# Feed-forward weight tiles placed by when the mixer's bytes come free, in a two-layer decoder trunk

## The chip, the cores and the metric
The kernel runs on one core of a Trainium2 chip. A core has a matrix engine (TensorE, PE in the profile; its weight loads are PEld), three engines for elementwise work (VectorE or DVE, ScalarE or ACT, GpSimd or POOL), and a queue engine that issues the transfers here (SyncE, SP). Each engine works through its own list of instructions in order and waits on semaphores for the others. The metric is the device time of one launch in microseconds (us).

## The reference
256 tokens of width 2048 pass through two layers. Each layer is a token mixer and a feed-forward network, both added to the residual stream after an RMS norm of their input; a last norm ends it. All is float32.

```python
def swiglu(x, w_in, w_out):
    g, u = jnp.split(x @ w_in, 2, axis=-1)
    return (jax.nn.silu(g) * u) @ w_out
# layer 0: h = h + mlstm_mixer(norm(h));  h = h + swiglu(norm(h), ...)
# layer 1: h = h + rglru_mixer(norm(h));  h = h + swiglu(norm(h), ...)
# w_in: 2048 x (2 x 5632), w_out: 5632 x 2048
```

Both mixers begin with projections of the normed input and end with a projection of 2048 to 2048 (`m_w_out`, `r_w_out`), whose result is added to the residual `h`.

## The kernel before, in words
TensorE multiplies float32 numbers in a rounded format, so each factor is split in a rounded part (hi, a cast on ScalarE) and the rest (lo, a subtraction on VectorE), and a product is three matmuls: hi x hi, hi x lo, lo x hi. Every weight comes from memory once, as a raw tile; ScalarE writes its `whi`, VectorE its `wlo`. All weight loads stand on SP, in the order of their use.

A mixer streams its weights in groups of 128 x 2 x 512 (lines 180 to 200), four buffers each for raw, hi and lo in a pool "w". Its last step is `project_out` (line 422): four quarters of 512 output columns, each a `linear_tok` (line 250) of 96 matmuls into two banks `po` (lines 258 to 260), then two adds to `h` (line 429). After each quarter the norm's work for the next part is put in a list: transposes of `h`, here `tr_f` (line 381), all through one bank, a copy with the norm's gain `c_f` (line 384), some differences (line 386) and the split of the result `p_f` (lines 206 and 207), and squares for the norm (`junk`, line 309). That of the fourth quarter (pairs 6 and 7 of the input) falls behind the projection. The transposes of the second mixer are `tr_m`, its scaled inputs `x_m`, its first projection `rec`.

A feed-forward network (`ffn`, line 671) works on 11 feature blocks j. Block j takes eight pairs of 128 input rows; for each a raw tile 128 x 4 x 512 (two loads: gate and value columns; line 233). Five pairs are plain: one cast `whi` of 128 x 2048, one subtraction `wlo`, 24 matmuls. Pairs 1, 3 and 5 use seven products instead of eight: VectorE makes sums of the raw tile (`sum`, lines 242 to 246), raw and sums are split (`whix`, `wlox`, `whit`, `wlot`), 21 matmuls. The matmuls are lines 687 to 689, into seven banks P1 to Q6, which the profile shows as `P` and `Q`. Two or three blocks of inner features (tiles `hh`, `hl`) are then projected back by `w_out`.

The tiles of a network's weights all come from one pool:

```python
def four(what, name, dtype, bufs):                        # line 202
    return pool_of("w").tile([P, 4, NB], dtype, tag=what, name=..., bufs=bufs)
```

four raw, one sum, three hi, three lo, of 8 KB a partition each. This pool is opened at the network's start (line 676), where the mixer's pools have been closed, and lies over their bytes; each tile waits for what last used those bytes (`reuse_waits="tile"`). The first raw tiles lie over the mixer's raw and hi buffers, the first `whi` over its lo buffers, the first `wlo` over the pool y. The bytes of the mixer's inner part lie above and are given back after the first quarter of its projection (`nxt.open()`, line 433); over them lies the pool "f" with the inner features.

The order of each engine's list is set by a scheduler, by priority and by when it expects tiles to be ready; splits run under `tc.high_priority(offset=AHEAD)` (lines 192, 222, 235, 240), so they are put as early as their tiles allow.

Of the kernel before, what the change touches and what calls it, by code (L numbers as in the profile page):

```python
# [9 lines left out]
F32R = mybir.dt.float32r  # L10
# [4 lines left out]
P = 128  # L15
T = 256
# [8 lines left out]
NB = 512  # L25
# [13 lines left out]
def kernel(  # L39
# [28 lines left out]
    def open_pool(key, name, bufs=1, side="left", space=None):  # L68
        kw = dict(space=space) if space is not None else dict(side=side)
        pool = tc.tile_pool(name=name, bufs=bufs, reuse_waits="tile", **kw)  # L70
        pools[key] = (pool.__enter__(), pool)
        return pools[key][0]

    def close_pools(*keys):
        for key in keys:
            pools.pop(key)[1].__exit__(None, None, None)

    def pool_of(key):
        return pools[key][0]

    def acc(name):
        return pool_of("acc").tile([P, NB], F32, tag="bank", name=name)

    def misc(name):
        return pool_of("misc" if "misc" in pools else "acc").tile([P, NB], F32, tag="bank", name=name)

    def open_mixer(n):
        open_pool("acc", f"acc_{n}", 8, space=PSUM)
        open_pool("w", f"w_{n}", 4)
        open_pool("y", f"y_{n}")  # L90
# [8 lines left out]
    h = const.tile([P, NT, D], F32, name="h")  # L99
    xv = x[0].rearrange("(b p) d -> p b d", p=P)  # L100
    raw0 = {}
# [48 lines left out]
    part, at, used = 0, 0, [0, 0, 0]  # L150
    for name, src, n in par_src:
        if part == 0 and at or at + n > P:
            part, at = part + 1, 0
# [21 lines left out]
    def run_pending():  # L175
        if pending:
            pending.pop(0)()


    def stream(w, c0, nk, ncols=NB):  # L180
# [5 lines left out]
        for kg in range(0, nk, 2):  # L186
# [12 lines left out]
            for i in range(2):  # L199
                yield kg + i, hi[:, i, 0:ncols], lo[:, i, 0:ncols]  # L200

    def four(what, name, dtype, bufs):
        return pool_of("w").tile([P, 4, NB], dtype, tag=what, name=f"{what}{name}", bufs=bufs)

    def split(hi, lo, src):
        nc.scalar.copy(hi, src)  # L206
# [20 lines left out]
    def pairs(w, j):  # L227

        wv = w.rearrange("(k p) n -> p k n", p=P)
        for p in range(NK // 2):  # L230
            raw = four("raw", f"{j}_{p}", F32, 4)
            for i, c0 in enumerate((j * NB, FF + j * NB)):
                nc.sync.dma_start(raw[:, 2 * i:2 * i + 2, :], wv[:, 2 * p:2 * p + 2, c0:c0 + NB])
            if p not in SEVENS:
                with tc.high_priority(offset=AHEAD):
                    both = halves(f"{j}_{p}", raw)
                yield p, both
                continue

            with tc.high_priority(offset=AHEAD):  # L240
                t = four("sum", f"{j}_{p}", F32, 1)
                nc.vector.tensor_tensor(
                    t[:, 0:2, :], raw[:, 1:3, :], raw[:, 3:4, :].broadcast_to([P, 2, NB]), op=ALU.add
                )
                nc.vector.tensor_tensor(t[:, 2, :], t[:, 0, :], raw[:, 2, :], op=ALU.add)
                nc.vector.tensor_tensor(t[:, 3, :], t[:, 2, :], raw[:, 0, :], op=ALU.add)
                both = halves(f"x{j}_{p}", raw, 3) + halves(f"t{j}_{p}", t)
            yield p, dict(zip(("B21", "B11", "B22", "T1", "T3", "T2", "T4"), both))
# [188 lines left out]
    def split_store(dst_hi, dst_lo, src):  # L437

        nc.scalar.copy(dst_hi, src)  # L439
        nc.vector.tensor_tensor(dst_lo, src, dst_hi.bitcast(F32), op=ALU.subtract)  # L440
# [230 lines left out]
    def ffn(layer, n, nxt):  # L671

        w = ffn_w_in[layer]
        open_pool("acc", f"acc_f{layer}", 7, space=PSUM)
        open_pool("misc", f"misc_f{layer}", 1, space=PSUM)
        open_pool("w", f"w_f{layer}")
        fp = open_pool("f", f"f{layer}")

        def opening():
            close_pools("x")  # L680
            open_pool("x", f"x_after{layer}", side="right")

        nxt.opening = opening
        if True:

            def product(o, a, b, start, stop):
                nc.tensor.matmul(o, lhsT=a[0], rhs=b[0], start=start, stop=False)  # L687
                nc.tensor.matmul(o, lhsT=a[0], rhs=b[1], start=False, stop=False)  # L688
                nc.tensor.matmul(o, lhsT=a[1], rhs=b[0], start=False, stop=stop)  # L689

            def hidden(j):

                ps = {c: acc(f"{c}_{j}") for c, _, _ in PRODUCTS}
                started = set()
                dif = fp.tile([P, 2, NB], F32, tag="dif", name=f"dif{j}")
                sg = fp.tile([P, NT, NB], F32, tag="sg", name=f"sg{j}")
                for p, ops in pairs(w, j):
                    if p not in SEVENS:

                        for c, side, a in (("Q5", 1, 1), ("P2", 0, 0), ("Q3", 1, 2), ("P4", 0, 1)):  # L700
                            for f in range(2):
                                product(ps[c], n.plain(p, f)[a], ops[2 * side + f], c not in started,
                                        p == NK // 2 - 1 and f == 1)
                                started.add(c)
                    else:
                        seven = n.seven(p)
                        for c, a, b in PRODUCTS:
                            product(ps[c], seven[a], ops[b], c not in started,
                                    p == SEVENS[-1] and c in ("P7", "P1", "Q6"))
                            started.add(c)  # L710
                    if p == SEVENS[-1]:
                        nc.scalar.copy(sg[:, 0, :], ps["P1"])
                        nc.vector.tensor_tensor(dif[:, 0, :], ps["Q6"], sg[:, 0, :], op=ALU.subtract)
                        nc.vector.tensor_tensor(dif[:, 1, :], ps["P7"], dif[:, 0, :], op=ALU.add)
                    if p > 0:
                        run_pending()
                v = fp.tile([P, NT, NB], F32, tag="v", name=f"v{j}")
                for b in range(NT):
                    nc.vector.tensor_tensor(v[:, b, :], ps["Q5"], dif[:, b, :], op=ALU.add)
                nc.vector.tensor_tensor(sg[:, 0, :], ps["P2"], sg[:, 0, :], op=ALU.add)  # L720
                nc.scalar.activation(sg[:, 0, :], sg[:, 0, :], AF.Silu, scale=n.rstd[:, 0:1])
                nc.vector.tensor_tensor(v[:, 0, :], ps["Q3"], v[:, 0, :], op=ALU.add)
                nc.vector.tensor_tensor(sg[:, 1, :], ps["P4"], dif[:, 1, :], op=ALU.subtract)
                nc.scalar.activation(sg[:, 1, :], sg[:, 1, :], AF.Silu, scale=n.rstd[:, 1:2])
                for b in range(NT):
                    nc.vector.scalar_tensor_tensor(
                        out=v[:, b, :], in0=v[:, b, :], scalar=n.rstd[:, b:b + 1], in1=sg[:, b, :],
                        op0=ALU.mult, op1=ALU.mult,
                    )
                return v  # L730

            def turn_v(v, i, hi, lo):
                pt = misc("tv").rearrange("p (f t) -> p f t", f=2)
                for f in range(2):
                    for b in range(NT):
                        nc.tensor.transpose(
                            pt[:, f, b * P:(b + 1) * P], v[:, b, (2 * i + f) * P:(2 * i + f + 1) * P], ident
                        )
                split_store(hi[:, 2 * i:2 * i + 2, :], lo[:, 2 * i:2 * i + 2, :], pt)

            for js in CHUNKS:
                hh, hl = [], []
                for i, j in enumerate(js):
                    v = hidden(j)
                    hi = fp.tile([P, 4, T], F32R, tag=f"hh{i}", name=f"hh{j}")
                    lo = fp.tile([P, 4, T], F32R, tag=f"hl{i}", name=f"hl{j}")
                    hh.append(hi)
                    hl.append(lo)
                    for a in range(2):
                        pending.append(lambda v=v, a=a, hi=hi, lo=lo: turn_v(v, a, hi, lo))  # L750
                project_out(
                    ffn_w_out[layer][js[0] * NB:(js[-1] + 1) * NB, :], 4 * len(js),
                    lambda k: (hh[k // 4][:, k % 4, :], hl[k // 4][:, k % 4, :]), nxt, js[-1] == FF // NB - 1,
                )

    n2 = Norm("m1", par["g_mix"][:, 16:32], bcast=True)
    ffn(0, n1, n2)
    close_pools("f", "w", "misc", "acc")
    open_mixer("m1")


# [165 lines left out]
            nc.sync.dma_start(ov[:, 2 * NB:4 * NB], y[:, 2 * NB:4 * NB])  # L927

    ffn(1, n3, Final("fin", None))
    close_pools("f", "w", "misc", "acc", "x")  # L930


# [29 lines left out]
```

## Time and profile before

| | us |
|---|---|
| runs | 2165.64, 2165.96, 2167.81; median 2165.96 |
| the profiled execution | 2165.18 |
| its span | 2163.4 |
| TensorE busy | 2126.7 |
| VectorE busy | 1524.6 |
| ScalarE busy | 1071.0 |
| mean granted clock of TensorE | 0.991 |

The span runs from the first to the last instruction of the profiled execution; 1.8 us of its time lie around it. Times in rows count from the span's start. A row of the timeline gives start, length, engine, line, operation, what is written and read, and how many alike were merged; in brackets the idle time of the engine before it and what ended it. The first network's products begin at 411.41, the second mixer's at 1134.72, the second network's at 1436.55.

### The profile page before, as it was taken

What the parts mean: (1) busy time and instruction counts of PE and PEld (TensorE: products, weight loads), DVE (VectorE), ACT (ScalarE), POOL (GpSimd) and SP (SyncE); (2) the same over time, 40 slices, a digit from 0 to 9 for tenths busy, and PEclk for the clock granted to TensorE, in tenths of its full rate; (3) what the DMA queues carried; (4) which work ended last, traced back from release to release, by engine and by line L of the source; (5) the groups of instructions that cost most, each with busy time, mean ns of one, the idle gap of its engine ahead of it and who ended that gap; (6) DMA issues with size and microseconds to landing.
All of it is one profiled execution on the core that took longest, in us unless ns stands there. A gap on an engine that the chain in (4) does not pass through costs nothing.

```text
span 2163.4 us, 26826 instructions
## 1 busy us (share of the span) xinstructions
PE 2126.7 (98%) x10658; PEld 1788.9 (83%) x10658; DVE 1524.6 (70%) x1486; ACT 1071.0 (50%) x1040; POOL 43.4 (2%) x62
## 2 busy tenths in 40 slices
PE   8999999899999999999999999989999999999998
PEld 7988888788888888888879999778888888888886
DVE  5655555688578758866856786768857875886685
ACT  5444445555345435544544758555434543553444
POOL 0011110000000000000000000000000000000002
PEclk9999999999999999999999999999999999999999
DMA  6556655556555655565636665555665565556563
GB/s 209 166 163 178 180 180 185 178 202 209 189 193 188 203 186 195 195 201 188 206 106 195 194 188 188 190 176 195 214 195 194 175 214 175 194 195 213 176 214 117
DMA packets 211078, 405.70 MB, mean 188 GB/s; under 512 B 14520, under 2 KB 14728, under 8 KB 210824
## 3 DMA queue, kind: packets, MB, share of 16 engines
q1 hardware_dynamic: 210808, 402.94, 57.2%
q8 instruction: 83, 1.36, 0.3%
q10 hardware_dynamic: 144, 1.05, 0.1%
q14 instruction: 43, 0.35, 0.0%
HBM read 401.84 MB, written 2.10 MB: 187 GB/s over the span
## 4 chain that ended last, share of the span: by engine, by line
PE 91%; DVE 3%; ACT 2%; DMA 2%; issue 1%; SPq 0%; POOL 0%; ACTq 0%; DVEq 0%; POOLq 0%
PE po L259 10%; PE po L258 10%; PE po L260 10%; PE P L688 7%; PE P L689 7%; PE P L687 7%; PE Q L688 6%; PE Q L689 6%; PE Q L687 6%; DMA raw<-in_ffn_w_in_dram 2%; PE rec L277 1%; PE qk L275 1%; DVE wlo L207 1%; PE qk L276 1%; PE rec L276 1%; PE o L260 1%
## 5 line engine op out<-in xcount | busy, mean ns | idle before, releaser
L206 ACT CAST whi<-raw 128x2048 fp32r<-128x2048 f32 x198 | 378.3, 1912 | 465.8 <-PE P L689 204.4
L207 DVE TENSOR_TENSOR wlo<-raw,whi 128x2048 fp32r<-128x2048 f32 x198 | 451.8, 2295 | 204.8 <-ACT whi L206 204.6
L196 DVE TENSOR_TENSOR wlo<-raw,whi 128x1024 fp32r<-128x1024 f32 (+1 forms) x225 | 273.3, 1219 | 194.0 <-ACT whi L195 193.7
L195 ACT CAST whi<-raw 128x1024 fp32r<-128x1024 f32 (+1 forms) x225 | 234.3, 1047 | 215.8 <-PE po L260 53.2
L259 PE MATMUL po<-wlo,hh 128*128 128x512 f32 x704 | 275.2, 391 | 0.0
L258 PE MATMUL po<-whi,hh 128*128 128x512 f32 x704 | 275.0, 391 | 0.0
L260 PE MATMUL po<-whi,hl 128*128 128x512 f32 x704 | 273.6, 390 | 0.0
L206 ACT CAST whit<-sum 128x2048 fp32r<-128x2048 f32 x66 | 126.2, 1913 | 161.5 <-PE P L689 94.5
L207 DVE TENSOR_TENSOR wlot<-sum,whit 128x2048 fp32r<-128x2048 f32 x66 | 151.3, 2292 | 58.9 <-ACT whit L206 58.7
L687 PE MATMUL Q<-whi,p_f 128*128 128x512 f32 x440 | 175.7, 399 | 8.5 <-ACT whi L206 8.5
L688 PE MATMUL Q<-wlo,p_f 128*128 128x512 f32 x440 | 174.1, 396 | 3.6 <-DVE wlo L207 3.6
L687 PE MATMUL P<-whi,p_f 128*128 128x512 f32 x440 | 174.0, 395 | 0.0
L689 PE MATMUL Q<-whi,p_f 128*128 128x512 f32 x440 | 172.8, 393 | 0.0
L688 PE MATMUL P<-wlo,p_f 128*128 128x512 f32 x440 | 172.7, 393 | 0.0
L689 PE MATMUL P<-whi,p_f 128*128 128x512 f32 x440 | 172.5, 392 | 0.0
L258 PEld LDWEIGHTS po<-whi,hh 128*128 128x128 f32 x704 | 132.2, 188 | 27.5 <-ACT hh L439 0.3
L259 PEld LDWEIGHTS po<-wlo,hh 128*128 128x128 f32 x704 | 132.5, 188 | 26.5
L260 PEld LDWEIGHTS po<-whi,hl 128*128 128x128 f32 x704 | 132.1, 188 | 26.9
L206 ACT CAST whix<-raw 128x1536 fp32r<-128x1536 f32 x66 | 98.0, 1485 | 80.6 <-PE P L689 53.9
L207 DVE TENSOR_TENSOR wlox<-raw,whix 128x1536 fp32r<-128x1536 f32 x66 | 115.7, 1753 | 16.8 <-ACT whix L206 16.3
L687 PEld LDWEIGHTS Q<-whi,p_f 128*128 128x128 f32 x440 | 83.4, 190 | 26.6 <-ACT whi L206 9.1
L688 PEld LDWEIGHTS Q<-wlo,p_f 128*128 128x128 f32 x440 | 83.3, 189 | 24.4 <-DVE wlo L207 7.4
(261 smaller groups left out, 4258.5 us busy)
## 6 DMA issues: line engine op xcount, KB each, us to landing
raw<-in_ffn_w_in_dram SPq DMA_DIRECT2D x352, 512.0 KB, 4.8
raw<-in_ffn_w_out_dram SPq DMA_DIRECT2D x176, 512.0 KB, 4.9
raw<-in_m_w_in_dram SPq DMA_DIRECT2D x95, 512.0 KB, 3.8
raw<-in_r_w_in_dram SPq DMA_DIRECT2D x64, 512.0 KB, 4.2
raw<-in_m_w_out_dram SPq DMA_DIRECT2D x32, 512.0 KB, 3.7
raw<-in_r_w_out_dram SPq DMA_DIRECT2D x32, 512.0 KB, 3.7
gr<-in_r_gate_w_dram SPq DMA_DIRECT2D x8, 512.0 KB, 3.8
h<-in_x_dram SPq DMA_DIRECT2D x4, 512.0 KB, 7.9
```

Source lines behind the costliest of these rows:

```text
L195: nc.scalar.copy(hi[:, i:i + step, 0:ncols], r)
L196: nc.vector.tensor_tensor(lo[:, i:i + step, 0:ncols], r, hi[:, i:i + step, 0:ncols].bitcast(F32), op=ALU.subtract)
L206: nc.scalar.copy(hi, src)
L207: nc.vector.tensor_tensor(lo, src, hi.bitcast(F32), op=ALU.subtract)
L258: nc.tensor.matmul(o, lhsT=ah[:, bs], rhs=hi, start=(k == 0), stop=False)
L259: nc.tensor.matmul(o, lhsT=ah[:, bs], rhs=lo, start=False, stop=False)
L260: nc.tensor.matmul(o, lhsT=al[:, bs], rhs=hi, start=False, stop=(k == nk - 1))
L275: nc.tensor.matmul(o, lhsT=hi, rhs=ah, start=first_in_bank, stop=False, skip_group_check=True)
L276: nc.tensor.matmul(o, lhsT=hi, rhs=al, start=False, stop=False, skip_group_check=True)
L687: nc.tensor.matmul(o, lhsT=a[0], rhs=b[0], start=start, stop=False)
L688: nc.tensor.matmul(o, lhsT=a[0], rhs=b[1], start=False, stop=False)
L689: nc.tensor.matmul(o, lhsT=a[1], rhs=b[0], start=False, stop=stop)
```

## The change
Every tile of the one pool "w" of a network gets a pool of its own, and these are opened in the order of a list. Since pools are laid out in the order of opening, the list sets which of the mixer's bytes each tile lies over. A counter for each kind takes the tiles in turn. The first raw, `whi` and `wlo` of a network are not taken from these but from the pool "f", from the tiles `h0`, `h1`, `h2`, which hold the inner features later. For that the hi and lo of a feature block, two tiles of 4 KB, become one of 8 KB. Lines below 205 move by 8 and lines behind 686 by 12: 206 and 207 are 214 and 215 in the changed kernel, 233 is 241, 687 to 689 are 699 to 701.

```diff
+    PLACES = ("raw0", "raw1", "raw2", "raw3", "sum0", "whi2", "whi0", "wlo0", "whi1", "wlo2", "wlo1")
+    turn, early = {}, {}
+
     def four(what, name, dtype, bufs):
-        return pool_of("w").tile([P, 4, NB], dtype, tag=what, name=f"{what}{name}", bufs=bufs)
+        if what in early:
+            return pool_of("f").tile([P, 4, NB], dtype, tag=early.pop(what), name=f"{what}{name}")
+        at = turn.get(what, 0)
+        turn[what] = (at + 1) % bufs
+        return pool_of(f"{what}{at}").tile([P, 4, NB], dtype, tag=what, name=f"{what}{name}")
...
-        open_pool("w", f"w_f{layer}")
+        turn.clear()
+
+        early.update(raw="h0", whi="h1", wlo="h2")
+        for place in PLACES:
+            open_pool(place, f"{place}_f{layer}")
         fp = open_pool("f", f"f{layer}")
...
-                    hi = fp.tile([P, 4, T], F32R, tag=f"hh{i}", name=f"hh{j}")
-                    lo = fp.tile([P, 4, T], F32R, tag=f"hl{i}", name=f"hl{j}")
+                    both = fp.tile([P, 2, 4, T], F32R, tag=f"h{i}", name=f"hh{j}")
+                    hi, lo = both[:, 0], both[:, 1]
...
-    close_pools("f", "w", "misc", "acc")
+    close_pools("f", *reversed(PLACES), "misc", "acc")
```

SP, in the first mixer's output projection; `raw_0` is the first pair of the first network, the other rows are the mixer's weights:

```order
 L107 DMA raw_3031<-in_m_w_out_dram 128x2x512
 L107 DMA raw_3058<-in_m_w_out_dram 128x2x512
+L241 DMA raw_0_3645<-in_ffn_w_in_dram 128x2x512 x2
 L107 DMA raw_3076<-in_m_w_out_dram 128x2x512
 L107 DMA raw_3124<-in_m_w_out_dram 128x2x512
...
 L107 DMA raw_3552<-in_m_w_out_dram 128x2x512
 L107 DMA raw_3570<-in_m_w_out_dram 128x2x512
-L233 DMA raw_0_3615<-in_ffn_w_in_dram 128x2x512 x2
```

The two loads move ahead of 23 of the mixer's 32 (in the second network ahead of 16). The cast `whi_0` of that tile moves likewise, into the projection's first quarter.

ScalarE behind the first mixer's end, before (in `whi_0`, `whix_1` and so on the number is that of the pair; `c_f_3687` and `p_f_3691` are those of pair 6, `c_f_3730` and `p_f_3734` of pair 7):

```order
L309 ACTIVATE junk,ss_f_211<-h 128x512 x2
L384 ACTIVATE c_f_3687<-tr_f_3682,cols_107 128x256 x2
L206 CAST p_f_3691<-c_f_3687 128x768
L384 ACTIVATE c_f_3730<-tr_f_3725,cols_107 128x256 x2
L206 CAST whi_0_3618<-raw_0_3615 128x2048
L206 CAST p_f_3734<-c_f_3730 128x768
L206 CAST whix_1_3653<-raw_1_3646 128x1536
L206 CAST whit_1_3657<-sum_1_3649 128x2048
L206 CAST whi_2_3697<-raw_2_3694 128x2048
```

And now (pair 6 is `c_f_3717` and `p_f_3721`, pair 7 `c_f_3760`):

```order
L317 ACTIVATE junk,ss_f_211<-h 128x512 x2
L214 CAST whix_1_3683<-raw_1_3676 128x1536
L392 ACTIVATE c_f_3717<-tr_f_3712,cols_107 128x256 x2
L214 CAST whi_2_3727<-raw_2_3724 128x2048
L214 CAST whit_1_3687<-sum_1_3679 128x2048
L214 CAST whix_3_3783<-raw_3_3776 128x1536
L214 CAST p_f_3721<-c_f_3717 128x768
L392 ACTIVATE c_f_3760<-tr_f_3755,cols_107 128x256 x2
L214 CAST whit_3_3787<-sum_3_3779 128x2048
L214 CAST whi_4_3815<-raw_4_3812 128x2048
```

The cast of pair 0 is gone from here, four casts of the weights of pairs 1 to 3 stand ahead of the split `p_f` of pair 6, and `whi_2` ahead of `whit_1`. On TensorE the 24 matmuls of pair 0 follow the last `po` matmul, where eight transposes stood; the transposes now stand, two or four at a time, between pair 1's matmuls. The start of the second network is alike.

TensorE at the end of the last quarter before the second mixer, now (`tr_m_8418` are the transposes of the third quarter's last part, `rec_0` is the second mixer's first projection):

```order
L266 MATMUL po_1_8382<-whi_8440,hh_8118 128x512
L331 MATMUL tr_m_8418<-ident,h 128x128 x4
L267 MATMUL po_1_8382<-wlo_8441,hh_8118 128x512
...
L268 MATMUL po_1_8382<-whi_8440,hh_8118 128x512
L283 MATMUL rec_0_8523<-x_m_8230,whi_8527 128x256
L284 MATMUL rec_0_8523<-x_m_8230,whi_8527 128x256
L285 MATMUL rec_0_8523<-x_m_8230,wlo_8528 128x256
L283 MATMUL rec_0_8523<-x_m_8230,whi_8527 128x256
```

These transposes stood at the third of the last 24 `po` matmuls and are now at the sixteenth, and 36 `rec` matmuls follow each other without transposes between. Ahead of it VectorE and ScalarE have the first four splits of the second mixer's weights (lines 195 and 196) before the last quarter's adds and squares, where they stood behind them.

## Rows read from the trace of the kernel before

**Rows 1.** The page, first part: busy time, share of the span, instructions.
```profile
PE 2126.7 (98%) x10658; PEld 1788.9 (83%) x10658; DVE 1524.6 (70%) x1486; ACT 1071.0 (50%) x1040; POOL 43.4 (2%) x62
```

**Rows 2.** Waits of TensorE: us in total, times, longest.
```profile
PE Q L687 <- ACT whi L206: 8.5, 2, 4.4
...
PE rec L275 <- ACT whi L195: 2.6, 1, 2.6
PE tr_f L381 <- ACT c_f L384: 2.0, 2, 1.0
```

**Rows 3.** Stretches: busy PE, PEld, DVE, ACT, POOL, then PEclk, DMA, GB/s.
```profile
408.00:412.00 4.00, 0.59 (x1) 0.50 (x2) 1.67 (x3) 3.26 (x5) 0.00 (x0) 0.50 0.84 318
...
418.00:420.00 2.00, 2.00 (x10) 1.62 (x10) 0.56 (x1) 1.40 (x1) 0.00 (x0) 1.00 0.29 35
...
1433.00:1437.00 4.00, 0.45 (x1) 0.45 (x2) 1.67 (x3) 3.13 (x4) 0.00 (x0) 0.50 1.05 395
...
1135.00:1138.00 3.00, 2.51 (x11) 2.13 (x11) 3.00 (x5) 2.51 (x3) 0.00 (x0) 0.50 0.14 10
...
1513.00:1516.40 3.40, 2.58 (x11) 1.80 (x10) 3.40 (x3) 2.20 (x2) 0.00 (x0) 1.00 0.05 6
```

**Rows 4.** Timeline of TensorE, the first network's start.
```profile
403.65 0.39 PE L260 MATMUL po<-whi,yl 128*128 128x512 f32 x1
...
406.38 0.66 PE L381 MATMUL tr_f<-ident,h 128*128 128x128 f32 x4 [1.01 <-ACT c_f L384]
411.41 0.80 PE L687 MATMUL Q<-whi,p_f 128*128 128x512 f32 x1 [4.38 <-ACT whi L206]
...
416.47 0.63 PE L689 MATMUL P<-whi,p_f 128*128 128x512 f32 x1
416.89 0.63 PE L687 MATMUL P<-whi,p_f 128*128 128x512 f32 x1
...
441.00 0.39 PE L687 MATMUL P<-whix,p_f 128*128 128x512 f32 x1
...
456.80 0.39 PE L687 MATMUL Q<-whi,p_f 128*128 128x512 f32 x1
```

**Rows 5.** Timeline of ScalarE, the first network's start.
```profile
404.88 0.63 ACT L309 ACTIVATE junk<-h 128x512 f32<-128x512 f32 x1
405.41 0.19 ACT L309 ACTIVATION_READ_ACCUMULATOR junk<-h 128x1 f32 x1
...
409.47 1.90 ACT L206 CAST whi<-raw 128x2048 fp32r<-128x2048 f32 x1
```

**Rows 6.** Timeline of VectorE, the first network's start.
```profile
411.39 2.29 DVE L207 TENSOR_TENSOR wlo<-raw,whi 128x2048 fp32r<-128x2048 f32 x1 [1.36 <-ACT whi L206]
413.60 1.22 DVE L242 TENSOR_TENSOR sum<-raw 128x1024 f32<-128x1024 f32 x1
```

**Rows 7.** Timeline of TensorE, the second network's start.
```profile
1428.79 0.39 PE L260 MATMUL po<-whi,zl 128*128 128x512 f32 x1
...
1481.88 0.39 PE L687 MATMUL Q<-whi,p_f 128*128 128x512 f32 x1
```

**Rows 8.** Timeline of TensorE, the second mixer's start.
```profile
1131.73 0.39 PE L260 MATMUL po<-whi,hl 128*128 128x512 f32 x1
1134.72 0.55 PE L275 MATMUL rec<-x_m,whi 128*128 128x256 f32 x1 [2.61 <-ACT whi L195]
...
1142.25 0.28 PE L277 MATMUL rec<-x_m,wlo 128*128 128x256 f32 x1
...
1142.59 0.28 PE L277 MATMUL rec<-x_m,wlo 128*128 128x256 f32 x1
```

**Rows 9.** Timeline of VectorE and ScalarE, the second mixer's start.
```profile
1131.47 1.37 DVE L429 TENSOR_TENSOR h<-po,h 128x512 f32<-128x512 f32 x2 [2.35 <-PE po L260]
...
1133.64 3.87 ACT L195 CAST whi<-raw 128x1024 fp32r<-128x1024 f32 x4
```

**Rows 10.** Timeline of ScalarE, inside the first mixer's output projection.
```profile
325.04 1.05 ACT L195 CAST whi<-raw 128x1024 fp32r<-128x1024 f32 x1 [1.67 <-PE po L260]
```

**Rows 11.** Timeline of VectorE, the same place.
```profile
326.12 1.22 DVE L196 TENSOR_TENSOR wlo<-raw,whi 128x1024 fp32r<-128x1024 f32 x1 [1.49 <-ACT whi L195]
```

**Rows 12.** The page, DMA issues: line, engine, count, KB each, us to landing.
```profile
raw<-in_m_w_out_dram SPq DMA_DIRECT2D x32, 512.0 KB, 3.7
```

More of the change, by code (lines that the diff above doesn't have):

```diff
@@ L929 @@
     ffn(1, n3, Final("fin", None))
-    close_pools("f", "w", "misc", "acc", "x")
+    close_pools("f", *reversed(PLACES), "misc", "acc", "x")
 _INS = [
```

## The prediction
> **What bounds the kernel now.** I read the page first. TensorE is busy for 98% of the span [rows 1], so only time in which TensorE stands still or runs slowly can be won. The list of what TensorE waits for is short [rows 2]. The longest entry is the first product of a feed-forward network that waits for its hi weights (8.5 us in two waits, one for each network); the first product of the second mixer waits 2.6 us for the same kind of cast, and transposes wait 2.0 us until their one bank has been read. The table of stretches shows the rest of the price [rows 3]: behind each of those three waits the granted clock reads 0.50, the lower of the two levels (1.2 GHz against 2.4 GHz), and comes back some microseconds after the matmuls resume. Such a stop is thus paid twice.
>
> The timelines give the size of each place. In the first network [rows 4] the last `po` matmul of the mixer starts at 403.65, eight transposes follow, the first product starts at 411.41 after a wait of 4.38 us, and its matmuls stand 0.42 us apart (416.47, 416.89) until the clock returns; afterwards they stand closer: from the start of pair 5 at 441.00 to that of the second feature block at 456.80 are 21 + 24 + 24 matmuls, 0.229 us each. Between lie 5 plain pairs of 24 matmuls and 3 pairs of 21, so 183 matmuls; at 0.229 us they need 41.9 us, and the eight transposes some 1.1 us more (four take 0.66 with their tail). From 403.88, where the next matmul could start, to 456.80 are 52.9 us. So 9.9 us are lost: 5.4 in the two waits that the rows show, 2.7 in 14 matmuls at the low clock, the rest in smaller waits and the restart. The second network is alike [rows 7]: 1429.02 to 1481.88 are 52.9 us, 9.9 lost. At the second mixer [rows 8] the last matmul starts at 1131.73 and the first 36 of the projection are done with by 1142.70, one pitch behind the row at 1142.59; 36 at 0.114 us (three from 1142.25 to 1142.59) need 4.1 us, so 6.6 are lost. All three together are 26.4 us, and that is the most that can be had here.
>
> Why the products are late is on ScalarE [rows 5]: the squares of the norm end at 405.60, then come the casts of the last two pairs of inputs, and only at 409.47 the cast of the first weight tile. It stands there because the tile it writes lies over the mixer's buffers.
>
> **The change part by part.** Nothing is added to the number of matmuls, splits or bytes; instructions move.
>
> (1) The first pair of a network now lies where the inner features will lie, over bytes of the mixer that are free after the first quarter of its output projection. Its two loads, its cast (1.90 us, [rows 5]) and its subtraction (2.29 us, [rows 6]) go into that projection. There ScalarE has an idle 1.67 us ahead of each cast of 1.05 us [rows 10], so a 1.90 us cast makes one cast late by about 0.3 us and the next ones on time again; if the weights land later than the cast's turn, up to some 3 us, which the four buffers of each kind (each group is 2.7 us of matmuls) cover. VectorE has 1.49 us ahead of each of its subtractions [rows 11]. Cost taken: 0; from both sides 0 and, without any cover, 1.9 + 2.3 us in each of two mixers, 8.4 us.
>
> (2) Then the 24 matmuls of pair 0 follow the last `po` matmul without a wait: 403.88 to 409.38. During them ScalarE does the squares and pair 1's cast and VectorE the sums of pair 1, which before began at 413.60 [rows 6] and now can at about 406.0. The wait of 4.38 us and the low clock behind it go.
>
> (3) What is late next. The transposes of pairs 6 and 7 now stand between the products of pair 1. The second four wait for the one bank as they do now, 1.01 us [rows 4]: pair 1's first three matmuls and four transposes end at 410.5, the wait at 411.5. Six more matmuls lead to 413.1. On ScalarE the cast of pair 2 (1.90) starts at 411.5 and ends at 413.4, a wait of 0.2; behind it the cast of pair 1's sums, of the same size, ends at 415.2, while TensorE has only two matmuls to do in between: a wait of 1.4. From there on 4 + 8 + 8 + 14 matmuls run to 423.0, where pair 3 starts; before, it started 114 matmuls of 0.229 us ahead of 456.80, at 430.7. Gain so far 7.7 us. In pairs 3 and 4 the sums, the cast of the sums and the next cast stand closer than now; by the same addition they make TensorE wait 0.2 + 0.95 + 0.15 us. So the second block starts at about 450.4 and 6.4 us are won in each network. As a check from VectorE: its series of sums starts 7.6 us earlier, so the gain in a network cannot be much over that unless VectorE has slack.
>
> (4) At the second mixer the first four splits of weights move ahead of the last quarter's squares and residual adds, because their buffers now lie over tiles that are let go earlier. Casts that stood at 1133.64 [rows 9] are then done before 1131.73, and rec can start as soon as its bank is free. That bank is one the last `po` tile's add reads; two adds take 1.37 us [rows 9], and the splits and the norm's last inputs are ahead of them now, so I put the first add's end at 1132.7 and TensorE's wait at 0.7 us, too short beside a long run of matmuls to expect the clock to fall. 1132.7 + 4.1 = 1136.8 against 1142.70: 5.9 us won.
>
> Sum: 6.4 + 6.4 + 5.9 = 18.7 us. The profiled execution took 2165.18 us (span 2163.4 and 1.8 around it), close to the median of 2165.96. 2165.2 - 18.7 = 2146.5.
>
> **The clock.** The assumption that carries 9 of the 18.7 us is that the new waits leave the clock up. In the rows it fell at three places, each time after TensorE had done nothing, or nothing but transposes, from the last matmul of a projection on; the shortest stop among them is the 2.61 us ahead of rec [rows 8]. The new waits are 1.0, 0.2 and 1.4 us with two to six matmuls between them, and in a stretch of the second network in which TensorE also had pauses (2.58 us busy of 3.40) the clock read 1.00 (the last of [rows 3]). So I take it to stay up, without a row that has just this pattern.
> The Trainium skill, page "TensorE: Matmul & The Clock Gate", section "A second HAM failure mode: psum-queue depth-cycling", tells of a kernel in which short pauses between groups of matmuls came often enough for the clock to go up and down, at the cost of throughput. By that rule the new start of a network would fall into the low clock again, which is rival (b); no row of before shows a fall after pauses as short as these.
>
> **The rivals.**
> (a) The waits vanish more fully than I add up: ScalarE takes the casts in time and the clock stays. Then each network wins 8 to 9 us and the mixer 6.5: 24 us, 2141 us. For it speaks that releases are not all at their latest; against it the order on ScalarE, in which three long casts follow the transposes.
> (b) The clock falls at the new pauses. 14 matmuls at 0.42 instead of 0.23 are 2.7 us [rows 4], with the restart about 3.5 for each network: 18.7 - 7 = 11.7 us, 2153.5. If the mixer's place falls too (36 matmuls of which some 24 at 0.21 instead of 0.11: 2.5 us), 2156.
> (c) The wait only moves: the splits of pairs 1 to 4 are the true limit, and TensorE waits for VectorE's series wherever pair 0 stands. Then only the low clock or little of it is won, under 4 us: 2162 to 2166. Against it: VectorE waits for ScalarE ahead of its first long subtraction [rows 6], so it isn't at its limit there.
> (d) Slower: the early cast holds ScalarE inside the mixer. ScalarE and VectorE take their work in order; if the cast of pair 0 waits for a load that is not there, every cast of the projection queues behind it, and TensorE runs dry about 3 us later. One quarter of the projection is eight such steps of 1.67 + 1.05 us, 21.8 us, so weights that come a whole quarter late would cost up to 18.8 us in each mixer. It decides the sign from 18.7 / 2 + 3, some 12.4 us of lateness in each. The loads stand among the mixer's own, which land in 3.7 us [rows 12], and what they wait for on TensorE ended with the mixer's inner part, so I give it little. At 15 us of lateness in each: 2165.2 - 18.7 + 2 x 12 = 2170.5.
>
> **How the numbers follow.** Forecast (2143 to 2150): 0.58. (a): 0.12. (b): 0.17. (c): 0.07. (d): 0.04; 0.02 is left for what I don't see, on either side. What a measurement can tell from no change is about 0.2%, 4.3 us; faster by more are the forecast, (a), (b) and a small part of (c): 0.89; the same, most of (c): 0.06; slower 0.05. The range for 8 times in 10 leaves out the far end of (a), part of (b), (c) and (d): 2139.5 to 2156.
>
> **What would show it.** In the profile after: the cast of a network's first weights some 80 us earlier than its first product, inside the projection, with no new wait of `po` behind it; the first product straight behind the last `po`; clock 1.00 through 404 to 424 of the first network; waits for c_f, whi and whit of about 1.0, 0.2 and 1.4 us in place of 4.4; the second block 6 us closer to the mixer's end; rec no more than 1 us behind the last `po`. A reading of 0.5 in these stretches would make (b) right, waits of `po` for ScalarE (d), and an unchanged distance from the mixer's end to the second block (c).

## The result, and the profile after
The changed kernel takes 2152.61 us (median of 4 runs, 2151.89 to 2154.57) against 2166.36 (4 runs, 2165.64 to 2167.81): a ratio of 0.9937, 95% interval 0.9920 to 0.9954. The forecast was 2146.5, so the sign and the range held, and 5 us of the forecast gain are missing. The profiled executions, 2165.18 and 2152.51 us, differ by 12.7 us. Cut at the same instructions (last `po` matmul, first matmul of the second feature block, last of the first 36 `rec`), in us:

| stretch | before | after | difference | forecast |
|---|---|---|---|---|
| start to the first mixer's end | 403.65 | 403.90 | +0.25 | 0 |
| first network, start to second block | 53.15 | 47.96 | -5.2 | -6.4 |
| rest of it | 674.93 | 675.79 | +0.9 | 0 |
| second mixer, first 36 `rec` | 10.86 | 5.13 | -5.7 | -5.9 |
| rest of it | 286.20 | 287.90 | +1.7 | 0 |
| second network, start to second block | 53.09 | 48.07 | -5.0 | -6.4 |
| rest and end | 681.5 | 682.0 | +0.4 | 0 |

The three places won 15.9 of the 18.7 us that were forecast for them, and 3.2 us went elsewhere. Of these 3.2, the +0.25 and the +0.9 do not come back when both kernels are profiled again (last experiment); the +1.7 does, and the +0.4 about does. What TensorE waits for now (us in total, times, longest):

```profile
PE Q L700 <- DVE wlo L215: 4.4, 6, 1.0
PE P L699 <- ACT whit L214: 4.3, 4, 1.1
PE tr_f L389 <- ACT c_f L392: 1.9, 2, 0.9
...
PE P L699 <- ACT whi L214: 1.0, 2, 0.5
...
PE rec L283 <- DVE h L437: 0.7, 1, 0.7
```

The two waits that led [rows 2], 8.5 us for whi and 2.6 for rec, are gone; new ones of at most 1.1 us stand in their place. The stretches at the three places (columns as in [rows 3]: the granted clock is the number before the DMA share):

```profile
408.00:412.00 4.00, 3.07 (x16) 2.29 (x15) 2.55 (x4) 1.04 (x3) 0.00 (x0) 1.00 1.02 346
414.00:416.00 2.00, 0.94 (x4) 0.48 (x3) 2.00 (x2) 2.00 (x2) 0.00 (x0) 1.00 0.45 172
...
1429.00:1433.00 4.00, 2.93 (x14) 2.09 (x13) 2.63 (x3) 4.00 (x3) 0.00 (x0) 1.00 0.65 248
1128.00:1132.00 4.00, 3.33 (x30) 3.31 (x30) 1.98 (x6) 1.84 (x5) 0.73 (x2) 1.00 0.52 186
```

All are at 1.00 where [rows 3] had 0.50. TensorE at the first network's start, after:

```profile
403.90 0.39 PE L268 MATMUL po<-whi,yl 128*128 128x512 f32 x1
404.13 0.39 PE L699 MATMUL Q<-whi,p_f 128*128 128x512 f32 x1
...
411.86 0.44 PE L389 MATMUL tr_f<-ident,h 128*128 128x128 f32 x2 [0.93 <-ACT c_f L392]
...
415.44 0.50 PE L699 MATMUL P<-whit,p_f 128*128 128x512 f32 x1 [1.06 <-ACT whit L214]
...
426.98 0.50 PE L699 MATMUL P<-whi,p_f 128*128 128x512 f32 x1 [0.48 <-ACT whi L214]
...
438.45 0.50 PE L699 MATMUL P<-whit,p_f 128*128 128x512 f32 x1 [1.06 <-ACT whit L214]
...
451.86 0.39 PE L699 MATMUL Q<-whi,p_f 128*128 128x512 f32 x1
```

The first product follows the last `po` without a gap; before, 7.8 us lay between [rows 4]. Four small waits remain. Behind each, the next matmuls stand 0.34 us apart once or twice instead of 0.23. ScalarE shows where the waits for `whit` come from:

```profile
410.96 0.84 ACT L392 ACTIVATE c_f<-tr_f,cols 128x256 f32<-128x256 f32 x2 [3.73 <-PE tr_f L389]
411.69 1.90 ACT L214 CAST whi<-raw 128x2048 fp32r<-128x2048 f32 x1
413.49 1.90 ACT L214 CAST whit<-sum 128x2048 fp32r<-128x2048 f32 x1
...
434.69 1.91 ACT L214 CAST whi<-raw 128x2048 fp32r<-128x2048 f32 x1 [5.64 <-PE P L701]
436.51 1.89 ACT L214 CAST whit<-sum 128x2048 fp32r<-128x2048 f32 x1
```

Ahead of both stands the cast of the next pair. The sums that the first `whit` casts were ready at 410.4, where VectorE's last addition for them ended; their cast started 3.1 us later, behind `c_f` and `whi`.

The early cast inside the mixer's projection, ScalarE and then VectorE:

```profile
325.83 1.91 ACT L214 CAST whi<-raw 128x2048 fp32r<-128x2048 f32 x1 [2.21 <-DMA raw<-in_ffn_w_in_dram]
327.65 1.99 ACT L195 CAST whi<-raw 128x1024 fp32r<-128x1024 f32 x2
```
```profile
327.78 2.29 DVE L215 TENSOR_TENSOR wlo<-raw,whi 128x2048 fp32r<-128x2048 f32 x1 [2.89 <-ACT whi L214]
329.99 3.49 DVE L196 TENSOR_TENSOR wlo<-raw,whi 128x1024 fp32r<-128x1024 f32 x3
```

The cast waits for its load, and two of the mixer's casts and three of its subtractions then follow back to back; before, each had idle time ahead of it [rows 10, 11]. TensorE has no wait in this projection; in that of the second mixer it has 1.3 us in three short ones, as before (1.2). The second mixer's start, against [rows 8]:

```profile
1127.65 0.39 PE L268 MATMUL po<-whi,hh 128*128 128x512 f32 x1
1128.72 0.36 PE L283 MATMUL rec<-x_m,whi 128*128 128x256 f32 x1 [0.68 <-DVE h L437]
...
1132.78 0.28 PE L285 MATMUL rec<-x_m,wlo 128*128 128x256 f32 x1
```

### The profile page after: what moved, and what is told of

It reads as the page before. It is cut to its first block, busy times and chain, and to the rows that moved or that the text cites. A ratio compares the mean times of both kernels' runs of the same rounds, so it can differ in the third digit from the quotient of the medians.

```text
span 2150.7 us, 26823 instructions
## 1 busy us (share of the span) xinstructions
PE 2120.3 (99%) x10658; PEld 1784.2 (83%) x10658; DVE 1523.7 (71%) x1486; ACT 1070.3 (50%) x1040; POOL 45.1 (2%) x62
## 5 line engine op out<-in xcount | busy, mean ns | idle before, releaser
L266 PE MATMUL po<-whi,hh 128*128 128x512 f32 x704 | 275.0, 391 | 0.0
L268 PE MATMUL po<-whi,hh 128*128 128x512 f32 x704 | 273.6, 390 | 0.0
L266 PEld LDWEIGHTS po<-whi,hh 128*128 128x128 f32 x704 | 132.2, 188 | 27.6 <-ACT hh L447 0.3
L268 PEld LDWEIGHTS po<-whi,hh 128*128 128x128 f32 x704 | 132.1, 188 | 26.8
L699 PEld LDWEIGHTS P<-whi,p_f 128*128 128x128 f32 x440 | 82.6, 188 | 20.3 <-ACT whi L214 2.5
```

The lines of the kernel that those rows point to most:

```text
L266: nc.tensor.matmul(o, lhsT=ah[:, bs], rhs=hi, start=(k == 0), stop=False)
L268: nc.tensor.matmul(o, lhsT=al[:, bs], rhs=hi, start=False, stop=(k == nk - 1))
```

## The experiments
Theory A, after the result: the two parts of the change are two causes. A network's start depends on the first pair alone; the second mixer's start depends on which tile of the network lies under its lo buffers, and the list of places decides that only together with the first pair's move. The rivals are named with each run. All medians and ratios are against runs of the kernel before on the same chip; for the first four runs that is 2167.47 us.

**The list of places alone.** The line that sends the first pair to `h0`, `h1`, `h2` is taken out:

```diff
-        early.update(raw="h0", whi="h1", wlo="h2")
```

> Only the list of places is kept; the first pair's tiles come from it like all others, not from the inner features' pool. Theory A (the start of a network depends on the first pair lying over bytes that are free early, and the start of the second mixer on which tiles happen to lie under its lo buffers, which the first pair's leaving shifts by one turn): nothing is won, 2164 to 2168 us; the first product waits 4 us for its hi cast in both networks with the clock at 0.50 behind it, and rec waits 2.6 us. Theory B (the order of the places itself lets the casts go earlier): 4 us or more in each network or 5 us at the second mixer, 2150 to 2161 us.

Measured: 2168.51 us against 2167.47, ratio 1.0000 (0.9991 to 1.0009). The networks' starts take 53.07 and 53.09 us. Its waits are those of before:

```profile
PE Q L698 <- ACT whi L214: 8.7, 2, 4.4
...
PE rec L283 <- ACT whi L195: 2.6, 1, 2.6
```

So the order of the places wins nothing by itself, neither at the networks nor at the second mixer. Theory B is out.

**The first pair alone.** The old pool "w" stays, and `four` has only the branch for the first pair:

```diff
     def four(what, name, dtype, bufs):
+        if what in early:
+            return pool_of("f").tile([P, 4, NB], dtype, tag=early.pop(what), name=f"{what}{name}")
         return pool_of("w").tile([P, 4, NB], dtype, tag=what, name=f"{what}{name}", bufs=bufs)
```

> The old single pool is kept; only the first pair of each network lies in the inner features' tiles. Theory A: each network's start to its second block takes 48 us as in the changed kernel (53.1 before), the second mixer's start stays as before (2.6 us wait, clock 0.50, 11 us for the first 36 matmuls): 2155 to 2158 us. Theory B: without the order of places the first pair alone wins under 2 us a network: 2162 or more. The cast of the sums of pairs 1 and 5 stands ahead of the next pair's cast here; if the reverse order costs time in the changed kernel, a network's start is 1 to 2 us shorter than there (46 to 47).

Measured: 2156.85 us, ratio 0.9947 (0.9933 to 0.9961); 47.53 and 47.54 us from the mixers' ends to the second blocks, rec with its old wait:

```profile
1127.80 0.39 PE L264 MATMUL po<-whi,hh 128*128 128x512 f32 x1
1130.79 0.39 PE L279 MATMUL rec<-x_m,whi 128*128 128x256 f32 x1 [2.61 <-ACT whi L195]
```

The networks' gain is the first pair's, all of it. With `whit` ahead of the next pair's `whi` on ScalarE a start is 0.5 us shorter than in the changed kernel, less than the 1 to 2 us that were expected: the wait moves to `whi` (1.8 us in three waits in the first network).

**Two places swapped.** In the changed kernel:

```diff
-    PLACES = ("raw0", "raw1", "raw2", "raw3", "sum0", "whi2", "whi0", "wlo0", "whi1", "wlo2", "wlo1")
+    PLACES = ("raw0", "raw1", "raw2", "raw3", "sum0", "whi1", "whi0", "wlo0", "whi2", "wlo2", "wlo1")
```

> The changed kernel with two places swapped (whi2 and whi1); the starts of the networks have the same order of instructions, but the second mixer's first four splits stand behind the last adds again. Theory A: the networks keep their 48 us, the second mixer's start goes back from 5.2 to 11 us: 5 to 6 us slower than the changed kernel, 2157 to 2159; if the slower pitch of the 256-column matmuls behind that start (0.118 for 0.113 us, 1.7 us in all) belongs to the new start, it goes with it, and the loss is 4. Theory B (the first pair's move alone makes room at the second mixer): no difference to the changed kernel, 2152 to 2154.

Measured: 2158.08 us, ratio 0.9953 (0.9941 to 0.9966). The networks' starts stay (48.08 and 48.07), the second mixer's goes back to 10.59:

```profile
1129.81 0.39 PE L268 MATMUL po<-whi,hh 128*128 128x512 f32 x1
1132.81 0.58 PE L283 MATMUL rec<-x_m,whi 128*128 128x256 f32 x1 [2.61 <-ACT whi L195]
```

So at the second mixer it counts which tile has the sixth place. A network makes 165 requests for a `whi` tile (11 in each of 11 blocks, 44 in the projections back), in turns of three. Without the first pair's own tile the last one is whi2; with it the counter has done 164 and the last one is whi1. The sixth place lies under the second mixer's lo buffers: whi2, which the changed kernel has there, was last used a quarter earlier if the first pair has left the turn, and is the last one used if it has not. The count and the places are read from the code and not from a trace; that neither part wins this alone, and that the swap undoes it, fits them.

**No stop, by useless work.** In the kernel before, 24 matmuls into a bank that is started anew later (`FILL` = 24), at the start of a network's first block:

```diff
+                if j == 0:
+                    for i in range(FILL):
+                        nc.tensor.matmul(ps["P4"], lhsT=n.x[0][:, 0, 0, :], rhs=n.x[0][:, 0, 0:4, :], start=(i == 0), stop=(i == FILL - 1))
```

> The kernel before with 24 more matmuls (5.5 us, into a bank that is started anew afterwards) behind the last matmul of each mixer, so that TensorE doesn't stop there; their result is used by nothing. The planner also puts the first weights' cast ahead of the inputs' casts. Theory A (a stop is paid twice, the second time by the low clock): the clock stays at 1.00, and from the mixer's end to the second block it takes 49 to 51 us in spite of 24 more matmuls, 2159 to 2163 us. Theory C (the clock falls for another reason, or costs next to nothing): 53 us or more, up to 58.6 where nothing is hidden: 2166 to 2177.

Measured: 2163.35 us, ratio 0.9978 (0.9968 to 0.9988): faster with 48 more matmuls, 11 us of TensorE's time, and just above the 2159 to 2163 of theory A. The starts take 50.47 and 50.49 us. The clock, TensorE and ScalarE at the first network:

```profile
405.00:409.00 4.00, 4.00 (x19) 3.33 (x18) 1.66 (x5) 3.25 (x5) 0.73 (x1) 1.00 1.04 372
409.00:413.00 4.00, 4.00 (x22) 3.07 (x22) 3.18 (x2) 1.71 (x3) 0.00 (x0) 1.00 1.03 368
```
```profile
404.97 0.39 PE L261 MATMUL po<-whi,yl 128*128 128x512 f32 x1
405.19 5.62 PE L698 MATMUL P<-p_f 128*128 128x512 f32 x24
410.65 0.60 PE L382 MATMUL tr_f<-ident,h 128*128 128x128 f32 x4
411.01 0.48 PE L688 MATMUL Q<-whi,p_f 128*128 128x512 f32 x1
```
```profile
406.20 0.64 ACT L310 ACTIVATE junk<-h 128x512 f32<-128x512 f32 x1
406.73 0.18 ACT L310 ACTIVATION_READ_ACCUMULATOR junk<-h 128x1 f32 x1
406.83 1.90 ACT L207 CAST whi<-raw 128x2048 fp32r<-128x2048 f32 x1
```

The clock stays at 1.00 where TensorE doesn't stop. There is a second finding, which I hadn't looked for: the first cast, which the planner had put right behind the squares, ran there without a wait, 1.86 us behind the start of the last `po` matmul. In the kernel before it started 5.8 us behind that ([rows 4, 5]). So there the tile and its bytes were not what it waited for at run time. It stood behind the inputs' casts in ScalarE's list. A cast that is 4 us earlier could by itself account for all of the 2.6 to 2.7 us won in a network, so this run does not show that the stop was paid a second time by the clock: theory A's times about came out, its reason stays unproven.

**Pair 1's raw tile and sums moved as well.** In the changed kernel, with `ds` one tile for `dif` and `sg`:

```diff
-    PLACES = ("raw0", "raw1", "raw2", "raw3", "sum0", "whi2", "whi0", "wlo0", "whi1", "wlo2", "wlo1")
+    PLACES = ("raw1", "sum0", "raw2", "raw3", "whi2", "wlo2", "whi0", "whi1", "wlo0", "wlo1", "raw0")
...
-        early.update(raw="h0", whi="h1", wlo="h2")
+        early.update(raw="h0", whi="h1", wlo="h2", sum="ds")
...
-                dif = fp.tile([P, 2, NB], F32, tag="dif", name=f"dif{j}")
-                sg = fp.tile([P, NT, NB], F32, tag="sg", name=f"sg{j}")
...
                     if p == SEVENS[-1]:
+                        ds = fp.tile([P, 4, NB], F32, tag="ds", name=f"ds{j}")
+                        dif, sg = ds[:, 0:2], ds[:, 2:4]
```

> The changed kernel with two more tiles of a network's first pairs moved: the raw tile of pair 1 takes the last place (over bytes that are free after the first quarter), and its sums take the tiles of dif and sg, which nobody needs before pair 5; the other places are put in an order that keeps the second mixer's first splits early. So the sums and the casts of pair 1 go into the projection and the transposes of pairs 6 and 7 stand behind pairs 1 and 2. Theory A (the 5 us a network that are still lost are waits for ScalarE and VectorE with pair 1's splits among the inputs' work): 43.3 to 45 us from the mixer's end to the second block instead of 48, the second mixer's start stays at 5.2, 2143 to 2147 us, or 1.6 more or less by the pitch behind it. Theory D (VectorE's work as a whole is the limit in the first block, so a wait only moves to a later pair): 47 to 48 us, 2151 to 2154.

Measured: 2144.17 us against 2167.96, ratio 0.9887 (0.9870 to 0.9903), the fastest of all. The starts take 43.40 and 44.02 us; TensorE has no wait for a cast left there, and only one for a subtraction (0.7 us for `wlo`, second network). The casts of pair 1 run inside the projection:

```profile
394.04 1.48 ACT L214 CAST whix<-raw 128x1536 fp32r<-128x1536 f32 x1
395.42 1.90 ACT L214 CAST whit<-sum 128x2048 fp32r<-128x2048 f32 x1
...
405.39 1.90 ACT L214 CAST whi<-raw 128x2048 fp32r<-128x2048 f32 x1
```

So most of what the changed kernel still lost in a network's start was pair 1's splits and sums among the inputs' work, not VectorE's work as a whole; theory D is out.

**Both kernels once more.** Unchanged, for second profiles.

> The kernel before, unchanged, for a second profile. If the pitch of the 256-column matmuls behind the second mixer's start (0.113 us before, 0.118 in the changed kernel for 48 us) belongs to the order of the instructions, it is 0.113 here; if it falls one way or the other by itself, 0.118 may show here, and 1.6 us of the difference between two profiles is chance.

> The changed kernel, unchanged, for a second profile. As for the kernel before: 0.118 us behind the second mixer's start if the pitch belongs to the order, 0.113 possible if it falls by itself. The starts of the networks and of the second mixer again 48, 48 and 5.2 us.

Measured: 2166.53 and 2151.61 us; the stretches 53.09, 10.88 and 53.10 us, and 48.05, 5.27 and 48.06. The rest of the first network takes 675.63 and 675.37 us here, so the +0.9 of the first two profiles was chance between executions, and so was the +0.25 ahead of the first mixer's end (404.07 and 402.88 here). The rest of the second mixer takes 286.21 and 287.90, again +1.7, and the end 681.8 and 682.3.

Behind the second mixer's start the mean pitch of 256-column matmuls from 1150 to 1160 is 0.113 us in both profiles of the kernel before and 0.118 in both of the changed one, so it seems to belong to the build. It does not belong to the order of the instructions there: the swap has the old order and 0.113; the list of places alone, the first pair alone and the useless work have the old order too and 0.118, and the run with pair 1 moved has 0.118.

The second profile of the kernel before also shows something of the clock's price. Behind the first network's stop of the same length the clock came back sooner; from 416 to 418, first profile and second:

```profile
416.00:418.00 2.00, 2.00 (x6) 1.57 (x5) 2.00 (x4) 0.00 (x0) 0.00 (x0) 0.50 1.03 397
416.00:418.00 2.00, 2.00 (x11) 1.63 (x10) 2.00 (x3) 0.00 (x0) 0.00 (x0) 1.00 1.01 385
```

Pair 1's first product, in the first profile and then in the second, and the second profile's further rows:

```profile
420.40 0.39 PE L687 MATMUL P<-whix,p_f 128*128 128x512 f32 x1
```
```profile
411.83 0.80 PE L687 MATMUL Q<-whi,p_f 128*128 128x512 f32 x1 [4.38 <-ACT whi L206]
...
419.52 0.39 PE L687 MATMUL P<-whix,p_f 128*128 128x512 f32 x1
...
422.27 0.40 PE L687 MATMUL P<-whit,p_f 128*128 128x512 f32 x1
422.79 0.51 PE L687 MATMUL P<-whi,p_f 128*128 128x512 f32 x1
...
457.16 0.39 PE L687 MATMUL Q<-whi,p_f 128*128 128x512 f32 x1
```

From the first product to pair 1 it took 7.69 us instead of 8.99 ([rows 4] for 411.41), a gain of 1.3 us. At the second block nothing of it was left: 45.33 us against 45.39. TensorE had only caught up with the splits, which kept their times: ScalarE wrote pair 2's `whi` until 422.73, and its first product started at 422.79, after a short pause.

```profile
420.83 1.90 ACT L206 CAST whi<-raw 128x2048 fp32r<-128x2048 f32 x1
```

So about half of the low clock in the first network cost nothing in the end. At the second mixer it did cost something: with the same wait of 2.61 us, the old order and a clock that was low for fewer matmuls, the first 36 `rec` took 9.94 us in the run with the list of places alone (13 of them at the wide pitch, 27 in the kernel before) and 9.90 in that with useless work, against 10.86 and 10.88.

## Why the prediction was right, and where it was off
**The mechanism.** Steps (1), (2) and (4) came out as written. (1): the early cast made two of the mixer's casts and three of its subtractions late, and TensorE's list of waits shows none of it. (2): pair 0 ran from 404.13 to 409.63. (4): the wait of rec is 0.68 us where 0.7 was forecast, and the first 36 are done 5.2 us behind the last `po`, as the sum had it (5.1).

**Step (3) was mis-sized behind the start of pair 3.** Up to there it holds to 0.1 us: 423.37, with a mixer that ended 0.25 later, against 423.0. That closeness is in part luck: the single waits were 0.93, none and 1.06 us where 1.0, 0.2 and 1.4 were forecast, and the wider pitch behind them, for which the forecast had nothing, made up for it. From there the forecast had 1.3 us of waits in pairs 3 and 4. Measured are 0.48 in pair 4 and 1.06 in pair 5, where `whi` stands ahead of `whit` a second time, and the wider pitch behind each; together 2.4 us. The second block came at 451.86 instead of 450.4. I had followed ScalarE's order to pair 4 and stopped there: 1.2 and 1.4 us of the missing gain.

**The forecast left out the rest of the program.** It put everything outside the three places at 0. +1.7 us is the pitch behind the second mixer's start: some 350 matmuls at 0.1178 instead of 0.1133 us are 1.6. Nothing in the rows of before pointed to that, and the forecast had no term for it. +0.4 goes with waits for `wlo` in the second network's later blocks (2.0 and 2.2 us in the two profiles before, 2.4 and 2.8 now). +0.9 and +0.25 are chance between executions: the second profiles have -0.3 and -1.2 in their place.

**The stop's second price was counted too high.** The prediction took the 2.7 us of the low clock in the first network as lost on top of the waits. In the second profile of the kernel before half of the low clock is gone, and the second block starts no sooner. So not all of the 2.7 could have been won by the clock alone; the splits behind the stop set the time there.

**The reason given for the late cast was wrong at run time.** The prediction said that it stood there because its tile lay over the mixer's buffers. The run with useless work shows that its bytes and its data were there 4 us earlier; it was late by its place in ScalarE's list. What the planner took for the tile's release, no run here shows. The forecast came out all the same, because the new tile changes that place.

**The rivals.** (b), the clock falling at the new pauses, did not happen: 1.00 through pauses of 0.48 to 1.07 us in both networks. The Trainium skill, page "TensorE: Matmul & The Clock Gate", section "A second HAM failure mode: psum-queue depth-cycling", tells of a kernel whose clock went up and down with short pauses between groups of matmuls; this trace does not show that at these lengths and numbers. (a) was too hopeful for this change, though the run with pair 1 moved too reached its size, 24 us. (c) is refuted by the 15.9 us won and by that run, (d) by the lists of waits in the two projections: none, and the same 1.3 us as before.

**What stays open.** Why the 256-column matmuls of the second mixer's first blocks run at one pitch in some builds and at another in others, at the same granted clock. How much of the stop's price in the kernel before is the clock: the two profiles of that kernel show that half of it was free in the first network, and no run takes away all of it and nothing else. How much of a network's gain the kernel before could have had without moving a tile, by putting the first weights' cast ahead of the inputs' casts in ScalarE's list: the run with useless work shows that the cast could run there, but it has 24 more matmuls as well, and no run has the new order alone.

## What to carry to other kernels
A stop of the matrix engine between two stages is best looked up in the order of the engine that it waits for: what stands ahead of the late instruction, and would it have been ready sooner? Tiles that are needed late in a stage are free room for what the stage needs first, and can hold it while the stage before still runs; do this for as many of the first pieces as the room holds, since the next piece's wait takes the place of the first's. Where tiles rotate, moving one of them out of the turn shifts which buffer is the last one used at the other end, so two such edits are to be tested together and apart.

## What the runs showed of the hardware that was not expected
At a granted clock of 1.00 a stream of 256-column matmuls, each with its own weights, ran at 0.1133 or at 0.1178 us each for some 40 us at a time, the same in two profiles of each of two builds. The first and the last of the same 192 matmuls (`gb`, the second mixer's next projection), before and then in the changed kernel:

```profile
1161.61 0.28 PE L275 MATMUL gb<-x_m,whi 128*128 128x256 f32 x1
...
1183.26 0.28 PE L277 MATMUL gb<-x_m,wlo 128*128 128x256 f32 x1
```
```profile
1152.57 0.28 PE L283 MATMUL gb<-x_m,whi 128*128 128x256 f32 x1
...
1175.07 0.28 PE L285 MATMUL gb<-x_m,wlo 128*128 128x256 f32 x1
```

They take 21.65 and 22.50 us. In all nine profiles this stretch has one of these two lengths, to 0.01 us: 21.65 in both of the kernel before and in the swap, 22.5 in the others. The first mixer has the slower pitch from about 90 to 110 us in every profile. And a kernel with 48 useless matmuls was 0.2% faster: its matrix engine no longer stopped at two places, and a cast came 4 us earlier there; the run does not part the two.
